# Out projection of a hybrid trunk step: tokens split as 282 and 238 columns, and one product for the high and the low half of the 238

## The chip, the cores and the metric

The kernel runs on one core of a Trainium2 chip. A core has a matrix engine (TensorE, PE in the profile, with PEld for its weight loads), three elementwise engines (VectorE = DVE, ScalarE = ACT, GpSimd = POOL), a sync engine that issues DMAs (SP), an on-chip memory of 128 partitions (SBUF) and an accumulator memory of eight banks of 512 f32 columns (PSUM), into which PE writes. The metric is the device time of one execution in microseconds; the median of three runs is given.

## The reference, cut to what matters

One layer of a hybrid decoder trunk for 512 prompt tokens and 8 sample tokens, all in f32: half-step SwiGLU FFN, a mixer of two head groups, a second half-step FFN, a final norm. The mixer ends with the out projection that the change concerns:

```python
    cat = jnp.concatenate([pool_out, y], axis=-1).astype(h.dtype)
    return cat @ w_out, new_pool, new_conv, h_new.astype(ssm_h0.dtype)
...
        h = h + 0.5 * _swiglu(_rms_norm(h, ffn1_norm[l]), ffn1_w_gate[l], ffn1_w_up[l], ffn1_w_down[l])
        m, p, c, s = _hybrid_mixer(_rms_norm(h, mix_norm[l]), st_pool[l], st_conv[l], st_ssm[l],
...
        h = h + m
        h = h + 0.5 * _swiglu(_rms_norm(h, ffn2_norm[l]), ffn2_w_gate[l], ffn2_w_up[l], ffn2_w_down[l])
```

The model width is 1024 and `w_out` is 1536 x 1024. `pool_out` (512 columns) comes from the pooling heads, `y` (1024) from the SSD heads: two groups of 512 columns, each gated with `silu(z)` and normed by its own RMS before the projection.

## The kernel before, in words

Features lie on the 128 partitions and the NT = 520 tokens on the columns. A product's output tile holds 128 features by up to 512 tokens, so the tokens are taken in two halves of HB = 260 (`HALVES`). To reach f32 accuracy with PE's faster f32r type, weights and inputs are split into a high part (the value rounded to f32r) and a low part (the rest), and each product is three: high weights by high input, high weights by low input, low weights by high input. Input tiles hold both halves, as `cat[:, q, k, tokens]` with q = 0 high, 1 low, and k one of four blocks of 128 features.

The out projection is the function `wout(cat, j, d2, fin)`. j = 0, 1, 2 is the third of the concat: the pooling heads (`catp`), then the two gated SSD groups (`cats[0]`, `cats[1]`; in the trace both are called catg). d2 = 0..3 is a weight unit of 1024 columns, good for two output blocks d of 128 features. For each d and each half b, a bank `wo{j}_{d}{b}` takes twelve products of 260 columns (`mm_low_last`: for four k the two with the high weights, then the four with the low weights), and then VectorE adds the bank to the residual `h[:, d, half]`. These are 3 x 8 x 2 = 48 groups, 576 products and 48 adds. In the last third, `fin` follows the add of the second half: ScalarE squares h for the next norm and scales the input of FFN2 (xg_f), which VectorE and ScalarE then split again into high (xth_f) and low (xtl_f).

Strings set the order in which the code issues the stages. `GATE_PLAN` mixes the thirds "o" (j = 0) and "g" (j = 1) with the rest of the SSD scan and the gates; `LAST_PLAN` is "h0 h2 h1 n0 h3 n1 n2 n3", with the last third (h) and pieces of FFN2's first unit in plain f32 between (n, `fill`; rows P<-xg_f at L311). Within this a scheduler orders each engine's instructions by readiness and priority when the kernel is built; on the chip every engine then runs its own list strictly in that order, and waits there for semaphores of the others. So an add's place in VectorE's list is fixed.

A bank is free for the next group when the adds that read it are done. In the mixer there are eight banks with the tag "ps", which the out projection shares with the scan. Before the last third the pool is released and FFN2's opened, with two banks "ps", two "A" and two pairs "BE"; the groups of the last third use the two "ps" banks in turn (d = 1 uses "A"), and the first of them wait for whatever stood in the same memory before.

What stands on VectorE around the adds: the splits of weights into low parts (rows tlo, wlo_wo, L141: 128x1024), the scan's X and E operations, decays of the sample states (h<-h,cb, L1144), two reciprocals of the gate's RMS (yr, L214) and the low halves of the gated concat (catg, L1339).

Of the kernel before, what the change touches and what calls it, by code (L numbers as in the profile page):

```python
# [13 lines left out]
ALU = mybir.AluOpType  # L14
# [7 lines left out]
NT = SEQ + NS  # L22
HB = NT // 2
HALVES = (slice(0, HB), slice(HB, NT))
KD = D // P
FFN = 2816
KF = FFN // P
# [32 lines left out]
_o = 0  # L60
for _n, _w in (("ffn1_norm", KD), ("mix_norm", KD), ("ffn2_norm", KD), ("final_norm", KD), ("pool_scale", 4),
               ("conv_w", 48), ("conv_b", 12), ("ssd_norm", NX), ("d_skip", NX), ("a_log", NX)):
# [6 lines left out]
def tile_trunk_step(ctx: ExitStack, tc: tile.TileContext, ins: dict, outs: dict):  # L69
    nc = tc.nc  # L70
# [9 lines left out]
    ps = [None]  # L80
# [3 lines left out]

    vx = act.tile([P, NVEC + KD * NT], F32, tag="h", name="h")
    vec = vx[:, :NVEC]
    h = vx[:, NVEC:].rearrange("p (d t) -> p d t", d=KD)

# [61 lines left out]
    def mm3(ps, whi, wlo, xhi, xlo, start, stop, pin=False, **kw):  # L150
# [3 lines left out]
        nc.tensor.matmul(ps, whi, xlo, start=False, stop=False, **kw)  # L154
        nc.tensor.matmul(ps, wlo, xhi, start=False, stop=stop, **kw)  # L155

    def mm_low_last(ps, whi, wlo, xhi, xlo, start, pin=False, **kw):
        for k, w in enumerate(whi):
            for x in (xhi[k], xlo[k]):
                mm = nc.tensor.matmul(ps, w, x, start=start, stop=False, **kw)  # L160
                if pin:
                    tc.keep_in_program_order(mm)
                start = pin = False
        for k, w in enumerate(wlo):
            nc.tensor.matmul(ps, w, xhi[k], start=False, stop=k == len(wlo) - 1, **kw)  # L165

    def ws(w, k, m=P):
        return w[:, k * m : (k + 1) * m]

    def stat(name):  # L170
        return (act.tile([P, NT], F32, tag="acc", name=f"acc_{name}"),
                act.tile([P, NT], F32, tag="r", name=f"r_{name}"))

    def new_x(xp, name):
        xh = xp.tile([P, KD, NT], F32R, tag="xa", bufs=2, name=f"xh_{name}")
        xl = xp.tile([P, KD, NT], F32R, tag="xa", bufs=2, name=f"xl_{name}")
        return xh, xl, *stat(name)
# [29 lines left out]
    def rstd(r, acc, hs, width, name, pin=False):  # L207
        ps = bank(f"psr_{name}")[:, : hs.stop - hs.start]
        for k, sq in enumerate(acc):
            mm = nc.tensor.matmul(ps, ones, sq, start=k == 0, stop=k == len(acc) - 1)  # L210
            if pin:
                tc.keep_in_program_order(mm)
        root = nc.scalar.activation(out=r[:, hs], in_=ps, func=AF.Sqrt, bias=eps, scale=1.0 / width)
        recip = nc.vector.reciprocal(out=r[:, hs], in_=r[:, hs])  # L214
        return root.ins, recip.ins

    def rstds(nx, name, pin=False):
        for b, hs in enumerate(HALVES):
            ends = rstd(nx[3], [nx[2][:, hs]], hs, D, f"{name}{b}", pin)
        return ends  # L220
# [4 lines left out]
    def new_xt(xp, name):  # L225
        return (xp.tile([P, KD // 2, 7, HB], F32R, tag="xth", name=f"xth_{name}"),
                xp.tile([P, KD // 2, 7, HB], F32R, tag="xtl", name=f"xtl_{name}"), *stat(name))
# [43 lines left out]
    class Ffn:  # L271
# [198 lines left out]
        def product(self, f, p):  # L470
# [22 lines left out]
            if self.i == 2:  # L493
                mm_low_last(out[:, :HB], wh, wl, *xs, opens, pin, skip_group_check=True)
            else:
                for j in js:
                    mm3(out[:, :HB], wh[j], wl[j], xs[0][j], xs[1][j], opens and j == 0, j == js[-1],
                        pin=pin and j == 0, skip_group_check=True)
# [93 lines left out]
        def down(self, c, lo, hi, after):  # L592
# [19 lines left out]
            def done(d):  # L612
# [6 lines left out]
                if after is None:  # L619
                    nc.vector.tensor_tensor(out=hd, in0=t, in1=hd, op=ALU.add)  # L620
                    return
                for b, hs in enumerate(HALVES):
                    nc.vector.tensor_tensor(out=h[:, d, hs], in0=t[:, b], in1=h[:, d, hs], op=ALU.add)
# [15 lines left out]
        def down_by_half(self, c, lo, after, wd):  # L639
# [32 lines left out]
            def done(d, b):  # L672
                hs = HALVES[b]
                t = self.wx.tile([P, 2, HB], F32, tag="ac", bufs=3, name=f"th{self.i}_{d}{b}")[:, 0]
                for c in QUARTERS if (d, b) == (KD - 1, 1) else (slice(0, HB),):
                    cs = slice(hs.start + c.start, hs.start + c.stop)
                    nc.vector.scalar_tensor_tensor(out=t[:, c], in0=banks[d, b][:, c], scalar=-0.5, in1=self.nx[3][:, cs],
                                                   op0=ALU.mult, op1=ALU.mult)
                    nc.vector.tensor_tensor(out=h[:, d, cs], in0=t[:, c], in1=h[:, d, cs], op=ALU.add)
                after(d, b, hs)  # L680
# [70 lines left out]
    nx2, xa = [], []  # L751
# [51 lines left out]

    ps[0] = tc.alloc_tile_pool(name="ppm", bufs=8, space=PSUM, reuse_waits="tile")
    mixer(tc, ins, outs, dict(locals()))
    f2["xg"].release()
    xa[0].release()
# [48 lines left out]
    def finish(b):  # L856
        hs, hg, rl, rt, idt = HALVES[b], *res
        acc = last[:, hs]
# [39 lines left out]
def mixer(tc, ins, outs, e):  # L898
    nc = tc.nc
    cst, act, wp, tmp, dr, pool = (e[x] for x in ("cst", "act", "wp", "tmp", "dr", "pool"))  # L900
    ones, queued, squared = e["ones"], e["queued"], tuple(e["added"])
    bank, load_unit, mm3, mm_low_last, ws, v, rstd, rstds, vec, h, nx2, raw_tile, open_f2, fin, fill = (
        e[x] for x in ("bank", "load_unit", "mm3", "mm_low_last", "ws", "v", "rstd", "rstds", "vec", "h", "nx2", "raw_tile",
                       "open_f2", "fin", "fill"))
    xh, xl, _, r = nx2[0]
    xa = e["xa"][0]
# [22 lines left out]
    def inproj(src, name):  # L929
        wh, wl = load_unit(src, D, f"in{name}", squared if name == "bc1" else ())  # L930
        bs = [bank(f"in{name}{b}") for b in range(2)]
        for b, hs in enumerate(HALVES):
            for k in range(KD):
# [18 lines left out]
    dtb = [bank(f"dt{b}") for b in range(2)]  # L952
    for b, hs in enumerate(HALVES):
        for k in range(KD):
# [331 lines left out]
    def wout(cat, j, d2, fin=None):  # L1286
        src, name = ins["w_out"][j, d2], f"wo{j}{d2}"
        if (j, d2) in OUT_LOW_BY_DMA:
            raw = raw_tile(name)
            nc.sync.dma_start(out=raw, in_=src)  # L1290
            wh, wl = e["weight_homes"](1024, name, wp, 3, ("whi", "wlo"))
            e["part_by_dma"](wh, wl, raw, src)
        else:
            wh, wl = load_unit(src, 1024, name, behind.get((j, d2), ()))
        for d in (2 * d2, 2 * d2 + 1):
            for b, hs in enumerate(HALVES):
                if d != 1 or j != 2:
                    ps = bank(f"wo{j}_{d}{b}")
                else:
                    ps = e["ps"][0].tile([P, 512], F32, tag="A", bufs=2, name=f"wo{j}_{d}{b}")  # L1300
                i = range((d % 2) * 4, (d % 2) * 4 + 4)
                mm_low_last(ps[:, :HB], *([ws(w, k) for k in i] for w in (wh, wl)),
                            *([cat[:, q, k, hs] for k in range(4)] for q in range(2)), True)
                nc.vector.tensor_tensor(out=h[:, d, hs], in0=ps[:, :HB], in1=h[:, d, hs], op=ALU.add)  # L1304
                if fin is not None:
                    fin(d, b, hs)

# [48 lines left out]
    def outs_a():  # L1356
# [19 lines left out]
        "B": lambda j: ssd_b(*ssd(j)),  # L1376
        "z": zproj,
        "o": lambda j: wout(catp, 0, j),
        "G": gate,
        "H": gate_out,  # L1380
        "g": lambda j: wout(cats[0], 1, j),
        "h": lambda j: wout(cats[1], 2, j, fin),
        "n": fill,
        "e": lambda j: outs_a(),
# [101 lines left out]
```

## Time and profile before

| what | value |
|---|---|
| runs | 956.82, 953.67, 954.66 us; median 954.66 |
| profiled execution, first to last instruction (its own time as the profile shows it) | 951.9 us, 2.76 below the median |
| granted TensorE clock, mean | 0.997 |
| PE / PEld busy | 942.5 us (99%) / 925.9 us (97%) |
| DVE / ACT / POOL busy | 852.7 (90%) / 635.7 (67%) / 148.3 us (16%) |
| out projection's adds (L1304) | 48, 19.2 us busy, from 532.2 to 609.3 us |
| out projection's products (L160, L165 wo) | from 525.5 to 608.5 us |

A row of a timeline gives the start, the time to the end of the last of the row's instructions, the engine, the line, the operation with output and inputs, the shape, how many (x), and in brackets how long the engine had been idle before and who released it. The duration of a single instruction is longer than the distance to the next one's start, since an engine begins the next before the last is through; the distance ("pitch") is what counts in a full engine. Profile times are those of one execution; the three runs have been timed without it.

### The profile page before, as it was taken

How to read it: one execution, taken by the hardware profiler on the slowest of the kernel's cores; microseconds unless marked ns; L12 is line 12 of the kernel's file. 1: busy time of each engine (PE TensorE's matmuls, PEld its weight loads, DVE VectorE, ACT ScalarE, POOL GpSimd, SP SyncE). 2: the span in 40 equal slices, each digit the busy share in tenths (PEclk: the TensorE clock that was granted, in tenths of full speed). 3: DMA queues.
4: the chain of work that ended last, by engine and by line, in shares of the span. 5: the costliest groups of instructions: out<-in, count | busy, mean ns of one | idle time of the engine just before them, and what ended most of it. 6: DMA issues, size and time to landing. Idle time of an engine off the chain costs nothing.

```text
span 951.9 us, 19681 instructions
## 1 busy us (share of the span) xinstructions
PE 942.5 (99%) x7674; PEld 925.9 (97%) x7674; DVE 852.7 (90%) x1462; ACT 635.7 (67%) x1179; POOL 148.3 (16%) x230
## 2 busy tenths in 40 slices
PE   9999999999999999999999999999999999999996
PEld 8999999999999999999999999999999999999996
DVE  6899899998988688789998998999999999999886
ACT  7777756677566455485668735777776676766774
POOL 0011100100100000046251100111112101122120
PEclk9999999999999999999999999999999999999998
DMA  7666554455553343354264453556666655776552
GB/s 205 187 166 150 143 151 135 115 140 156 134 155 95 86 134 122 92 180 138 91 184 133 141 114 115 138 122 160 163 173 176 163 146 144 171 194 185 145 180 91
DMA packets 53995, 138.35 MB, mean 145 GB/s; under 512 B 7750, under 2 KB 15878, under 8 KB 53902
## 3 DMA queue, kind: packets, MB, share of 16 engines
q1 hardware_dynamic: 39918, 104.19, 34.2%
q0 software_dynamic: 13712, 32.78, 18.7%
q8 instruction: 60, 0.98, 0.4%
q14 instruction: 33, 0.27, 0.1%
q10 hardware_dynamic: 272, 0.13, 0.0%
HBM read 129.74 MB, written 7.34 MB: 144 GB/s over the span
## 4 chain that ended last, share of the span: by engine, by line
PE 44%; DVE 2%; issue 1%; POOL 1%; DMA 1%; ACT 1%; DVEq 0%; ACTq 0%; POOLq 0%
PE A L160 8%; PE BE L160 6%; PE wo L160 5%; PE A L165 4%; PE BE L165 3%; PE wo L165 2%; PE P L311 1%; PE dh L155 1%; PE dh L151 1%; PE dh L154 1%; POOL zs L1068 1%; PE inz L151 1%; PE inz L154 1%; PE inz L155 1%; DMA room<-in_state_ssm 1%
## 5 line engine op out<-in xcount | busy, mean ns | idle before, releaser
L504 ACT COPY ac<-A 128x260 f32<-128x260 f32 x85 | 31.6, 372 | 35.4 <-PE A L155 17.3
L433 DVE TENSOR_TENSOR s<-raw 128x1024 f32<-128x1024 f32 x39 | 47.6, 1222 | 4.4 <-DMA raw<-in_w2gu 2.8
L504 ACT COPY ac<-BE 128x260 f32<-128x260 f32 x41 | 15.4, 376 | 33.6 <-PE BE L165 17.7
L151 PE MATMUL inx<-xh_mx,whi_inx 128*128 128x260 f32 x112 | 31.8, 284 | 0.0
L154 PE MATMUL inx<-xl_mx,whi_inx 128*128 128x260 f32 x112 | 31.6, 282 | 0.0
L155 PE MATMUL inx<-xh_mx,wlo_inx 128*128 128x260 f32 x112 | 31.6, 282 | 0.0
L1027 DVE SCALAR_TENSOR_TENSOR A<-U,h,A 128x544 f32<-128x544 f32 x36 | 29.0, 807 | 1.6 <-ACT A L1025 1.2
L311 PE MATMUL P<-x,raw 128*128 128x260 f32 x128 | 28.9, 385 | 0.2 <-DMA raw<-in_w1gu 0.2
L311 PEld LDWEIGHTS P<-x,raw 128*128 128x128 f32 x128 | 24.4, 192 | 4.2 <-DMA raw<-in_w1gu 0.6
L160 PE MATMUL wo<-catg,whi_wo 128*128 128x260 f32 x192 | 27.4, 285 | 0.0
L1193 ACT ACTIVATE so<-br,sxdt 128x128 f32<-128x128 f32 x64 | 22.8, 376 | 5.8 <-DVE room L1195 5.2
L160 PEld LDWEIGHTS wo<-catg,whi_wo 128*128 128x128 f32 x192 | 24.8, 188 | 0.2
L139 ACT CAST thi<-raw 128x1024 fp32r<-128x1024 f32 (+1 forms) x14 | 14.2, 1012 | 15.7 <-PE wo L160 4.8
L1304 DVE TENSOR_TENSOR h<-wo,h 128x260 f32<-128x260 f32 x48 | 19.2, 422 | 5.0 <-PE wo L165 4.7
L252 DVE TENSOR_TENSOR gs<-gq,gs 128x780 fp32r<-128x780 f32 (+1 forms) x28 | 23.3, 831 | 0.0
L151 PE MATMUL inz<-xh_mx,whi_inz 128*128 128x260 f32 x80 | 23.0, 287 | 0.0
L154 PE MATMUL inz<-xl_mx,whi_inz 128*128 128x260 f32 x80 | 22.7, 284 | 0.0
L155 PE MATMUL inz<-xh_mx,wlo_inz 128*128 128x260 f32 x80 | 22.6, 283 | 0.0
L251 ACT CAST gs<-gq 128x780 fp32r<-128x780 f32 (+1 forms) x28 | 20.6, 735 | 1.2 <-DVE gq L555 0.8
L151 PEld LDWEIGHTS inx<-xh_mx,whi_inx 128*128 128x128 f32 x112 | 21.1, 188 | 0.2 <-issue 0.2
L160 PE MATMUL A<-xth_f,qs 128*128 128x260 f32 x84 | 21.2, 283 | 0.0
L160 PE MATMUL A<-xtl_f,qs 128*128 128x260 f32 x84 | 21.2, 284 | 0.0
(3140 smaller groups left out, 4382.9 us busy)
## 6 DMA issues: line engine op xcount, KB each, us to landing
raw<-in_w2gu SPq DMA_DIRECT2D x44, 512.0 KB, 4.4
raw<-in_w1gu SPq DMA_DIRECT2D x41, 512.0 KB, 4.3
raw<-in_w_in SPq DMA_DIRECT2D x24, 512.0 KB, 3.7
raw<-in_w1d SPq DMA_DIRECT2D x16, 512.0 KB, 4.6
raw<-in_w2d SPq DMA_DIRECT2D x16, 512.0 KB, 4.6
raw<-in_w_out SPq DMA_DIRECT2D x12, 512.0 KB, 3.5
ab<-scr_acs SPq DMA_DIRECT2D x8, 512.0 KB, 5.5
h<-in_state_ssm SPq DMA_DIRECT2D x16, 256.0 KB, 3.7
```

What stands on the lines that cost most here:

```text
L151: first = nc.tensor.matmul(ps, whi, xhi, start=start, stop=False, **kw)
L154: nc.tensor.matmul(ps, whi, xlo, start=False, stop=False, **kw)
L155: nc.tensor.matmul(ps, wlo, xhi, start=False, stop=stop, **kw)
L160: mm = nc.tensor.matmul(ps, w, x, start=start, stop=False, **kw)
L165: nc.tensor.matmul(ps, w, xhi[k], start=False, stop=k == len(wlo) - 1, **kw)
L251: cast = nc.scalar.copy(hi, s)
L252: low = nc.vector.tensor_tensor(out=lo, in0=s, in1=hi.bitcast(F32), op=ALU.subtract)
L311: mm = nc.tensor.matmul(self.banks[f, u][b][:, :HB], ws(self.raw[f][:, u], j + 4 * q), xg[:, slot[q]], start=j == q == 0, stop=j == 3 and ...
L433: nc.vector.tensor_tensor(out=s1, in0=diag, in1=up0, op=ALU.add)
L504: self.copied = nc.scalar.copy(keep, out[:, :HB]).ins
L1027: nc.vector.scalar_tensor_tensor(out=A[:, :n], in0=U[:, j : j + n], scalar=w(j), in1=A[:, :n], op0=ALU.mult, op1=ALU.add)
L1193: nc.scalar.activation(out=o[:, q], in_=br, func=AF.Copy, scale=sxdt[:, j, b : b + 1]))
```

## The change

The tokens of the out projection are no longer cut at 260 but at 282 (`SPANS`, `WIDE`, `NARROW` = 238). The first part is computed as before with 282 columns. For the second part one product takes the high weights with the high and the low half of the rows side by side, 2 x 238 = 476 columns into one bank (`mm_both_low_last`), and the four low weights' products of 238 columns are added onto the first 238 of these. The bank then holds two partial sums, and VectorE adds the one and then the other to `h`. So a pair of halves has 20 products and not 24, with the same 6,240 columns, and three adds and not two. Of the rest of the kernel only line numbers change: `mm_low_last` is L176 and L181 now, `mm_both_low_last` L186 and L188, the adds L1332; `mm_both` and `join` are defined and not called.

```diff
--- before.py
+++ after.py
@@ -22,6 +22,9 @@
 NT = SEQ + NS
 HB = NT // 2
 HALVES = (slice(0, HB), slice(HB, NT))
+WIDE = 282
+NARROW = NT - WIDE
+SPANS = (slice(0, WIDE), slice(WIDE, NT))
 KD = D // P
 FFN = 2816
 KF = FFN // P
@@ -154,6 +157,19 @@
         nc.tensor.matmul(ps, whi, xlo, start=False, stop=False, **kw)
         nc.tensor.matmul(ps, wlo, xhi, start=False, stop=stop, **kw)

+    def mm_both(ps, whi, wlo, x, start, stop, pin=False):
+
+        n = x.shape[-1]
+        first = nc.tensor.matmul(ps[:, : 2 * n].rearrange("p (q t) -> p q t", q=2), whi, x, start=start, stop=False)
+        if pin:
+            tc.keep_in_program_order(first)
+        nc.tensor.matmul(ps[:, :n], wlo, x[:, 0], start=False, stop=stop)
+
+    def join(ps, home):
+        n = home.shape[-1]
+        nc.scalar.copy(home, ps[:, n : 2 * n])
+        return nc.vector.tensor_tensor(out=ps[:, :n], in0=ps[:, :n], in1=home, op=ALU.add)
+
     def mm_low_last(ps, whi, wlo, xhi, xlo, start, pin=False, **kw):
         for k, w in enumerate(whi):
             for x in (xhi[k], xlo[k]):
@@ -163,6 +179,13 @@
                 start = pin = False
         for k, w in enumerate(wlo):
             nc.tensor.matmul(ps, w, xhi[k], start=False, stop=k == len(wlo) - 1, **kw)
+
+    def mm_both_low_last(ps, whi, wlo, x):
+        n = x[0].shape[-1]
+        for k, w in enumerate(whi):
+            nc.tensor.matmul(ps[:, : 2 * n].rearrange("p (q t) -> p q t", q=2), w, x[k], start=k == 0, stop=False)
+        for k, w in enumerate(wlo):
+            nc.tensor.matmul(ps[:, :n], w, x[k][:, 0], start=False, stop=k == len(wlo) - 1)

     def ws(w, k, m=P):
         return w[:, k * m : (k + 1) * m]
@@ -899,8 +922,8 @@
     nc = tc.nc
     cst, act, wp, tmp, dr, pool = (e[x] for x in ("cst", "act", "wp", "tmp", "dr", "pool"))
     ones, queued, squared = e["ones"], e["queued"], tuple(e["added"])
-    bank, load_unit, mm3, mm_low_last, ws, v, rstd, rstds, vec, h, nx2, raw_tile, open_f2, fin, fill = (
-        e[x] for x in ("bank", "load_unit", "mm3", "mm_low_last", "ws", "v", "rstd", "rstds", "vec", "h", "nx2", "raw_tile",
+    bank, load_unit, mm3, mm_both, join, mm_low_last, mm_both_low_last, ws, v, rstd, rstds, vec, h, nx2, raw_tile, open_f2, fin, fill = (
+        e[x] for x in ("bank", "load_unit", "mm3", "mm_both", "join", "mm_low_last", "mm_both_low_last", "ws", "v", "rstd", "rstds", "vec", "h", "nx2", "raw_tile",
                        "open_f2", "fin", "fill"))
     xh, xl, _, r = nx2[0]
     xa = e["xa"][0]
@@ -1293,15 +1316,20 @@
         else:
             wh, wl = load_unit(src, 1024, name, behind.get((j, d2), ()))
         for d in (2 * d2, 2 * d2 + 1):
-            for b, hs in enumerate(HALVES):
+            for b, hs in enumerate(SPANS):
                 if d != 1 or j != 2:
                     ps = bank(f"wo{j}_{d}{b}")
                 else:
                     ps = e["ps"][0].tile([P, 512], F32, tag="A", bufs=2, name=f"wo{j}_{d}{b}")
                 i = range((d % 2) * 4, (d % 2) * 4 + 4)
-                mm_low_last(ps[:, :HB], *([ws(w, k) for k in i] for w in (wh, wl)),
-                            *([cat[:, q, k, hs] for k in range(4)] for q in range(2)), True)
-                nc.vector.tensor_tensor(out=h[:, d, hs], in0=ps[:, :HB], in1=h[:, d, hs], op=ALU.add)
+                if b:
+                    mm_both_low_last(ps, *([ws(w, k) for k in i] for w in (wh, wl)), [cat[:, :, k, hs] for k in range(4)])
+                else:
+                    mm_low_last(ps[:, :WIDE], *([ws(w, k) for k in i] for w in (wh, wl)),
+                                *([cat[:, q, k, hs] for k in range(4)] for q in range(2)), True)
+                n = hs.stop - hs.start
+                for q in range(1 + b):
+                    nc.vector.tensor_tensor(out=h[:, d, hs], in0=ps[:, q * n : q * n + n], in1=h[:, d, hs], op=ALU.add)
                 if fin is not None:
                     fin(d, b, hs)
```

How it stands on VectorE in the first third (o0), where the first adds meet the scan's X operations; wo0_01 is the bank of third 0, block d = 0, second half. Before:

```order
L1304 TENSOR_TENSOR h_69<-wo0_00_6668,h_69 128x260
L1304 TENSOR_TENSOR h_69<-wo0_01_6682,h_69 128x260
L1276 SCALAR_TENSOR_TENSOR X_4306<-X_4306,h_69,E21_6344 128x128 x4
L1144 TENSOR_TENSOR h0_61_6649<-h0_61_6649,cb61_6647 128x512
L1144 TENSOR_TENSOR h0_71_6658<-h0_71_6658,cb71_6656 128x512
L1304 TENSOR_TENSOR h_69<-wo0_10_6696,h_69 128x260
L1304 TENSOR_TENSOR h_69<-wo0_11_6710,h_69 128x260
L141 TENSOR_TENSOR tlo_3833<-raw_74,thi_3832 128x1024
```

Now:

```order
L1332 TENSOR_TENSOR h_69<-wo0_00_6668,h_69 128x282
L1332 TENSOR_TENSOR h_69<-wo0_01_6682,h_69 128x238
L1299 SCALAR_TENSOR_TENSOR X_4306<-X_4306,h_69,E21_6344 128x128 x4
L1167 TENSOR_TENSOR h0_61_6649<-h0_61_6649,cb61_6647 128x512
L1167 TENSOR_TENSOR h0_71_6658<-h0_71_6658,cb71_6656 128x512
L1332 TENSOR_TENSOR h_69<-wo0_01_6682,h_69 128x238
L1332 TENSOR_TENSOR h_69<-wo0_10_6693,h_69 128x282
L1332 TENSOR_TENSOR h_69<-wo0_11_6707,h_69 128x238
L144 TENSOR_TENSOR tlo_3833<-raw_74,thi_3832 128x1024
```

The second part of wo0_01 does not follow the first but stands behind the X operations and the two decays.

VectorE around the last low halves of the second gated concat (catg1, L1339 and now L1367), which the last third multiplies. Before:

```order
L1304 TENSOR_TENSOR h_69<-wo1_50_7153,h_69 128x260
L1304 TENSOR_TENSOR h_69<-wo1_51_7167,h_69 128x260
L1304 TENSOR_TENSOR h_69<-wo1_60_7186,h_69 128x260
L1339 SCALAR_TENSOR_TENSOR catg1_7109<-zs_5724,h_69,catg1_7109 128x520 x2
L1304 TENSOR_TENSOR h_69<-wo1_61_7200,h_69 128x260
L1339 SCALAR_TENSOR_TENSOR catg1_7109<-zs_5724,h_69,catg1_7109 128x520 x2
L141 TENSOR_TENSOR tlo_3833<-raw_74,thi_3832 128x1024
L1304 TENSOR_TENSOR h_69<-wo1_70_7214,h_69 128x260
L1304 TENSOR_TENSOR h_69<-wo1_71_7228,h_69 128x260
L141 TENSOR_TENSOR wlo_wo21_7400<-raw_74,whi_wo21_7399 128x1024
L1304 TENSOR_TENSOR h_69<-wo2_00_7267,h_69 128x260
```

Now:

```order
L1332 TENSOR_TENSOR h_69<-wo1_60_7144,h_69 128x282
L1367 SCALAR_TENSOR_TENSOR catg1_7073<-zs_5724,h_69,catg1_7073 128x520 x2
L1332 TENSOR_TENSOR h_69<-wo1_61_7158,h_69 128x238
L1367 SCALAR_TENSOR_TENSOR catg1_7073<-zs_5724,h_69,catg1_7073 128x520
L1332 TENSOR_TENSOR h_69<-wo1_51_7128,h_69 128x238
L1367 SCALAR_TENSOR_TENSOR catg1_7073<-zs_5724,h_69,catg1_7073 128x520
L144 TENSOR_TENSOR tlo_3833<-raw_74,thi_3832 128x1024
L1332 TENSOR_TENSOR h_69<-wo1_70_7169,h_69 128x282
L1332 TENSOR_TENSOR h_69<-wo1_71_7183,h_69 128x238
L1332 TENSOR_TENSOR h_69<-wo1_61_7158,h_69 128x238
L144 TENSOR_TENSOR wlo_wo21_7340<-raw_74,whi_wo21_7339 128x1024
L1332 TENSOR_TENSOR h_69<-wo1_71_7183,h_69 128x238
```

The second part of wo1_51 has come between the last two low halves, and the second part of wo1_61 stands behind the low part of a weight (tlo) and two more adds.

PE at the second group of the last third, wo2_01. Before:

```order
L160 MATMUL wo2_00_7267<-catg1_7109,whi_wo20_7263 128x260 [waits DVE_49]
L165 MATMUL wo2_00_7267<-catg1_7109,wlo_wo20_7264 128x260 x4
L160 MATMUL wo2_01_7281<-catg1_7109,whi_wo20_7263 128x260 x8
L165 MATMUL wo2_01_7281<-catg1_7109,wlo_wo20_7264 128x260 x4
L160 MATMUL wo2_10_7296<-catg1_7109,whi_wo20_7263 128x260 [waits DVE_49]
```

Now:

```order
L176 MATMUL wo2_00_7219<-catg1_7073,whi_wo20_7215 128x282 [waits DVE_49]
L181 MATMUL wo2_00_7219<-catg1_7073,wlo_wo20_7216 128x282 x4
L186 MATMUL wo2_01_7233<-catg1_7073,whi_wo20_7215 128x476 [waits DVE_49,PE_49]
L186 MATMUL wo2_01_7233<-catg1_7073,whi_wo20_7215 128x476 x3
L188 MATMUL wo2_01_7233<-catg1_7073,wlo_wo20_7216 128x238 x4
```

The group had no wait of its own; now its first product waits for VectorE, and by the value of the semaphore for the second part of wo1_61. In the first third, the first product of wo0_20 waits in the same way for the second part of wo0_01 (before, for its only add), and in the last third a narrow block waits for both parts of the block two before in its bank. On PE outside the out projection only a few pieces of the fills (P<-xg_f) move behind the next product's group; POOL's and SP's lists are the same, and on ACT a few neighbours change places.

## The prediction

> **What bounds the kernel now.** I read the page first, then the busy time by stretches of 10 us around the out projection (525 to 610 us), then PE and VectorE there in order of time. The page gives the span and the engines' shares:
>
> ```profile
> span 951.9 us, 19681 instructions
> PE 942.5 (99%) x7674; PEld 925.9 (97%) x7674; DVE 852.7 (90%) x1462; ACT 635.7 (67%) x1179; POOL 148.3 (16%) x230
> ```
>
> PE is busy 942.5 of 951.9 us, so over the whole program the time is the sum of PE's work: whatever makes PE stop is added, and shorter PE work is gained. The same by stretches (columns: stretch, length, busy time and number of instructions of PE, PEld, DVE, ACT, POOL, then the granted clock, the DMA share and GB/s):
>
> ```profile
> 530.00:540.00 10.00, 10.00 (x83) 8.95 (x82) 10.00 (x17) 9.66 (x26) 1.19 (x1) 1.00 0.30 90
> 540.00:550.00 10.00, 10.00 (x86) 10.00 (x85) 10.00 (x26) 7.25 (x12) 0.90 (x1) 1.00 0.57 157
> 550.00:560.00 10.00, 10.00 (x86) 10.00 (x85) 10.00 (x19) 4.39 (x6) 0.85 (x1) 1.00 0.74 175
> 560.00:570.00 10.00, 10.00 (x83) 9.88 (x82) 7.94 (x12) 1.79 (x3) 0.00 (x0) 1.00 0.19 61
> 570.00:580.00 10.00, 10.00 (x86) 10.00 (x85) 10.00 (x19) 4.60 (x6) 0.00 (x0) 1.00 0.26 77
> 580.00:590.00 10.00, 10.00 (x78) 9.71 (x77) 6.81 (x12) 6.55 (x9) 0.00 (x0) 1.00 0.44 135
> ```
>
> The stage that is changed has two full engines: PE 10.00 in every row, and VectorE (DVE) 10.00 in four of six. Its only air is 10 − 7.94 = 2.06 us and 10 − 6.81 = 3.19 us. The change makes PE's instructions fewer and DVE's more, so it must be costed on both.
>
> **PE's side.** For each pair of halves (24 of them) 24 products of 260 columns become 12 of 282, 4 of 476 and 4 of 238. Columns: 24 × 260 = 6,240, and 12 × 282 + 4 × 476 + 4 × 238 = 6,240. Only a price per product, not per column, can be saved. PE in order of time, and the dt projection with its narrow weights:
>
> ```profile
> 553.94 1.12 PE L160 MATMUL wo<-catg,whi_wo 128*128 128x260 f32 x8
> 554.90 0.64 PE L165 MATMUL wo<-catg,wlo_wo 128*128 128x260 f32 x4
> 555.37 1.12 PE L160 MATMUL wo<-catg,whi_wo 128*128 128x260 f32 x8
> ...
> L957 PEld LDWEIGHTS dt<-xh_mx,whi_w x16: 120/121/123, 351.8 to 355.9; 128*48 128x48 f32 x16
> L956 PEld LDWEIGHTS dt<-xl_mx,whi_w x14: 94/94/98, 352.1 to 355.7; 128*16 128x16 f32 x14
> ...
> 352.31 0.28 PE L957 MATMUL dt<-xh_mx,whi_w 128*48 128x260 f32 x1
> 352.43 0.28 PE L956 MATMUL dt<-xl_mx,whi_w 128*16 128x260 f32 x1
> 352.55 0.28 PE L957 MATMUL dt<-xh_mx,whi_w 128*48 128x260 f32 x1
> ...
> 584.91 1.91 PE L311 MATMUL P<-xg_f,raw 128*128 128x260 f32 x8
> ...
> 608.51 3.67 PE L311 MATMUL P<-xg_f,raw 128*128 128x260 f32 x16
> ```
>
> A group of twelve takes 555.37 − 553.94 = 1.43 us, 119 ns for one 260-column product, or 0.46 ns a column. The plain f32 products of the fills (L311, each recorded as two) take (3.67 − 1.91) / 8 = 220 ns a record of 260 columns. If such a record is two passes of the columns, one pass is 110 ns, and the other 9 to 10 ns of the 119 are a price per product. With 48- and 16-column weights (loads of 121 and 94 ns) the pitch is still 120 ns, so the weight load does not set it. Saved are 96 products × 0 to 10 ns = 0 to 1 us. I take the upper end, 40 ns a pair, since the two kinds of product differ by just that; it counts only where PE isn't made to wait afterwards. The Trainium skill ("TensorE: Matmul & The Clock Gate", Back-to-back issue gap) gives an isolated product N / 2.4 + 2.5 ns, by which 96 fewer would save 0.24 us and a 260-column product would take 110.8 ns; the trace's 119 speaks against those figures here.
>
> **DVE's side.** 48 adds of 260 columns become 24 of 282 and 48 of 238. The two parts of a narrow block are added in turn, the second reads the h that the first wrote. DVE at the first groups, and two dependent operations later:
>
> ```profile
> 530.99 0.68 DVE L1269 TENSOR_TENSOR hst<-pst,hst 128x512 f32<-128x512 f32 x1
> 531.59 0.68 DVE L1273 TENSOR_TENSOR E<-yd,E 128x512 f32<-128x512 f32 x1
> 532.19 0.75 DVE L1304 TENSOR_TENSOR h<-wo,h 128x260 f32<-128x260 f32 x2
> 532.86 1.91 DVE L1276 SCALAR_TENSOR_TENSOR X<-X,h,E 128x128 f32<-128x128 f32 x4
> 534.70 1.28 DVE L1144 TENSOR_TENSOR h<-h,cb 128x512 f32<-128x512 f32 x2
> 535.90 0.75 DVE L1304 TENSOR_TENSOR h<-wo,h 128x260 f32<-128x260 f32 x2
> 536.57 1.21 DVE L141 TENSOR_TENSOR tlo<-raw,thi 128x1024 fp32r<-128x1024 f32 x1
> ...
> 602.91 0.42 DVE L240 SCALAR_TENSOR_TENSOR xd_f<-xd_f,xg_f 128x260 f32<-128x260 f32 x1
> 603.37 0.43 DVE L242 SCALAR_TENSOR_TENSOR xd_f<-xd_f,xg_f 128x260 f32<-128x260 f32 x1
> ```
>
> Two adds take 536.57 − 535.90 = 0.67, one 0.335 to 0.338; 512 columns from a bank take 531.59 − 530.99 = 0.60. The slope is 0.265 / 252 = 1.05 ns a column, so an add of 282 costs 0.361 and one of 238 0.315. New DVE work: 24 × 0.361 + 48 × 0.315 − 48 × 0.338 = +7.6 us, against 5.25 us of air. Where the parts are neighbours, the second costs up to 603.37 − 602.91 − 0.338 = 0.12 more. Until its second part is added, the narrow block's bank isn't free.
>
> *First stop, o0.* In the order, the second part of block 1 of d=0 stands behind four X operations and two decays of h, and the third pair's first product now waits for it. Those end at 535.90, the widths shift that by (0.361 + 0.315 − 0.67) = 0, and the second part ends a duration of 0.40 later (a 260 shows 0.75 − 0.335 = 0.42): 536.30. PE began that group here:
>
> ```profile
> 535.11 1.23 PE L160 MATMUL wo<-catp,whi_wo 128*128 128x260 f32 x8
> ```
>
> So PE stops for 536.30 − 535.11 = 1.2 us. Nothing hides it; PE's order is fixed there. Bounds: 0, if a bank were free after all, and 1.3 with two savings of 40 ns ahead of it.
>
> *Second stop, the start of the last third.* Here DVE's three pauses, the end of the second gated concat, and the two products that need it:
>
> ```profile
> 562.75 0.43 DVE L1304 TENSOR_TENSOR h<-wo,h 128x260 f32<-128x260 f32 x1 [0.46 <-PE wo L165]
> 564.17 0.43 DVE L1304 TENSOR_TENSOR h<-wo,h 128x260 f32<-128x260 f32 x1 [1.00 <-PE wo L165]
> 565.20 3.42 DVE L214 RECIPROCAL yr<-yr 128x260 f32<-128x260 f32 x2 [0.60 <-ACT yr L213]
> ...
> 575.40 1.42 DVE L1339 SCALAR_TENSOR_TENSOR catg<-zs,h,catg 128x520 fp32r<-128x520 f32 x2
> 576.74 1.22 DVE L141 TENSOR_TENSOR tlo<-raw,thi 128x1024 fp32r<-128x1024 f32 x1
> 577.88 0.76 DVE L1304 TENSOR_TENSOR h<-wo,h 128x260 f32<-128x260 f32 x2
> ...
> 576.31 1.12 PE L160 MATMUL wo<-catg,whi_wo 128*128 128x260 f32 x8
> 577.75 1.11 PE L160 MATMUL wo<-catg,whi_wo 128*128 128x260 f32 x8
> ```
>
> Ahead of the third reciprocal stand 24 adds before, 12 of 282 and 24 of 238 now: 12 × 0.361 + 24 × 0.315 − 24 × 0.338 = 3.78 us later, of which the pauses 0.46 + 1.00 + 0.60 = 2.06 take up: 1.72. From there to the last low half of the concat 6 adds become 3 wide and 5 narrow ones: 3 × 0.361 + 5 × 0.315 − 6 × 0.338 = 0.63. DVE reaches the low of the next weight 2.35 late, at 579.09. The first group (576.31) waits for the last low half and is about 2.4 late. The second (577.75) now waits for a bank that falls free only with the second part of the sixth block, behind that weight low (577.88 − 576.74 = 1.14), a wide and a narrow add and its own 0.40: 579.09 + 1.14 + 0.36 + 0.31 + 0.40 = 581.30, 3.55 us after 577.75. This lateness is absolute: the first stop and PE's savings up to here lie in it.
>
> *Behind it.* Eight more pairs, less the first group, save about 7 × 0.040 = 0.3 us. Near the end, with two banks in turn, the last block waits for both parts of the block two before: its two adds and the split of 128x1024 between them (1.15) take 0.17 + 0.315 + 1.13 + 0.40 = 2.0 us, while the product between gives 1.44: +0.56. The last block's h, from which FFN2's first input is scaled and split, is complete one narrow add (0.315) and one operation put between (0.46, the pitch at 602.91) later: +0.8. FFN2 follows at a full PE, and nothing is made up there. Instructions of POOL and SP keep their order, and ACT's move by a place; their cost is 0, with their waits for DVE counted above.
>
> Sum: 3.55 − 0.3 + 0.56 + 0.8 = **+4.6 us**. The profiled execution is 951.9 long and goes to 956.5; the median of the runs, 954.66, lies 2.76 above that span, so the time is 959.3. Ends: lower +2.9 (the second stop only the first group's 2.4, half the tail), upper +9 (all 24 second parts 0.12 dearer, 2.9 us, and 1.5 of the 2.06 us of pauses not usable, since PE, for which DVE waits there, is late itself).
>
> **The rivals.**
> *A, the adds are mostly hidden.* For it: DVE's 3.19 us between 580 and 590, and the wait at 577.75 that only pays if no bank is free. Then the tail and a piece of the second stop remain, 0 to +2.8: 955 to 957.4. Against it: DVE's 10.00 in the three rows from 530 to 560.
> *B, faster: PE's pitch is set per product, by the weight load, not by columns.* PEld is at 97%. Then 282 and 238 cost 119 as 260 does, a 476 what its columns take, 476 × 110 / 260 = 201: a pair costs 16 × 119 + 4 × 201 = 2,708 ns and not 24 × 119 = 2,856, with 24 × 148 = 3.6 us saved: 951.1. It decides only if DVE stops PE for less than about 0.7 us. Against it: the dt rows, whose light loads gain nothing. The Trainium skill says in the same section that in a stream of loads and products both set the spacing, with about 81 ns at 128 columns and 131 at 512; an estimate by a straight line between these gives 6.2 us saved, but also 98 ns at 260, where the trace has 119.
> *C, a 238-column product runs at a lower rate.* No f32r product here is narrower than 260 columns, so the price is bounded by the plain f32 product, 2 × 220 ns for 260: at that rate a 238 costs 2 × 220 × 238 / 260 = 403 and not 109, 96 × 0.294 = +28 us, and DVE, with more time, stops PE no more: 982. At half the rate, 96 × 0.10 = +10: 965. Nothing in the profile speaks for it, and nothing excludes it.
>
> **How the numbers follow.** The measurement can tell about 0.3%, 2.9 us: below 951.8 is faster, above 957.5 slower. My case (957.5 to 963.7) gets 0.72, A 0.09, B 0.05, C 0.14 (most of it at the full f32 price). Slower is my case and C, 0.86; same is A, 0.09; faster is B, 0.05. The range 955.5 to 966 holds my case, most of A and the half rate of C, 0.8 together.
>
> **What would show it.** PE: a first gap ahead of the third pair of o0 of about 1.2 us released by an add of 238; gaps of 2 to 4 us in all at the first two groups of the last third; DVE at 10.00 from 530 to 580; pitches near 129, 212 and 107 ns for 282, 476 and 238. Adds near 0.44 and 0.40 long. I am wrong if PE runs through these places, if the 238 products stand 200 ns or more apart, or if PE's time for a pair falls by more than 0.1 us.

## The result and the profile after

The changed kernel takes 959.58 us (median of 4 runs, 958.80 to 963.15) and the kernel before 954.16 us beside it (4 runs). The ratio is 1.0058 with a 95% interval from 1.0035 to 1.008: 5.4 us slower, between 3.3 and 7.6. Taken again in the first group of experiments, the ratio was 1.0046 (1.0033 to 1.0059), 4.4 us. The forecast was 959.3, +4.6 us. One execution of e6 below took 1544.76 us at a granted clock of 0.556, where all others had 0.993 or more; the ratios leave it out, and without it e6's median is 956.58 and not 956.96.

The execution that was profiled first is not a typical one: its span is 961.3 us, the spans of the other three runs are 956.9 to 958.4. Part of that lies outside the change. It had lost 1.5 us before the out projection began, and 1.2 us behind it, at 675 us in FFN2, to a weight transfer that took 8.7 us where 4.2 is usual. So I read the terms from a second profile of the same kernel (e1 below), whose span is 956.1. Its page, first lines:

```profile
span 956.1 us, 19529 instructions
PE 943.8 (99%) x7578; PEld 923.9 (97%) x7578; DVE 859.5 (90%) x1486; ACT 635.4 (66%) x1179; POOL 148.4 (16%) x230
```

PE has 96 instructions fewer and is not less busy (943.8 against 942.5); VectorE (DVE) has 24 more and is 6.8 us busier. The busy time by stretches, of the profile taken first, shows PE below 10.00 where it was full in every row before:

```profile
530.00:540.00 10.00, 7.79 (x58) 6.24 (x58) 10.00 (x20) 9.10 (x23) 1.08 (x1) 1.00 0.23 67
...
560.00:570.00 10.00, 10.00 (x69) 9.51 (x68) 10.00 (x22) 3.00 (x5) 0.00 (x0) 1.00 0.33 105
570.00:580.00 10.00, 10.00 (x70) 9.54 (x69) 10.00 (x17) 3.54 (x5) 0.00 (x0) 1.00 0.18 55
580.00:590.00 10.00, 8.73 (x59) 8.07 (x58) 8.32 (x16) 4.04 (x6) 0.00 (x0) 1.00 0.31 105
```

VectorE's air between 560 and 570 (7.94 before) is gone. PE in order of time, from e1: the rows with an idle time in brackets are all its stops between 500 and 620 us.

```profile
536.17 1.27 PE L176 MATMUL wo<-catp,whi_wo 128*128 128x282 f32 x8 [1.37 <-DVE h L1332]
...
578.09 1.27 PE L176 MATMUL wo<-catg,whi_wo 128*128 128x282 f32 x8 [0.29 <-DVE h L1332]
...
580.88 1.11 PE L186 MATMUL wo<-catg,whi_wo 128*128 128x476 f32 x4 [0.98 <-DVE h L1332]
...
611.12 1.11 PE L186 MATMUL wo<-catg,whi_wo 128*128 128x476 f32 x4 [0.48 <-DVE h L1332]
```

All four are released by an add (L1332), at the third pair of o0, the first two groups of the last third and the last block (block here means one half of the tokens for one d). A bracket holds only what remains of a wait after PE's modelled end, so the sum of the brackets, 3.1, is less than what was lost; the starts tell the loss. VectorE beside them, from e1, with the adds that release the first three stops:

```profile
535.64 1.06 DVE L1332 TENSOR_TENSOR h<-wo,h 128x238 f32<-128x238 f32 x3
...
577.55 0.40 DVE L1332 TENSOR_TENSOR h<-wo,h 128x238 f32<-128x238 f32 x1
577.87 0.75 DVE L1367 SCALAR_TENSOR_TENSOR catg<-zs,h,catg 128x520 fp32r<-128x520 f32 x1
578.54 1.22 DVE L144 TENSOR_TENSOR tlo<-raw,thi 128x1024 fp32r<-128x1024 f32 x1
579.67 1.07 DVE L1332 TENSOR_TENSOR h<-wo,h 128x282 f32<-128x282 f32 x3
```

The first add of the group at 535.64 is the second part of o0's first narrow block; PE starts at 536.17, when it is through. The add at 577.55 is the second part of wo1_51; it ends at 577.95 and PE starts at 578.09. The third of the group at 579.67 is the second part of wo1_61; it ends at 580.74 and PE starts at 580.88.

### The profile page after: what moved, and what is told of

Read it like the earlier page. It is cut to its first block, busy times and chain, and to the rows that moved or that the text cites. A ratio compares the mean times of both kernels' runs of the same rounds, so it can differ in the third digit from the quotient of the medians.

```text
span 961.3 us, 19529 instructions
## 1 busy us (share of the span) xinstructions
PE 945.5 (98%) x7578; PEld 924.2 (96%) x7578; DVE 859.2 (89%) x1486; ACT 635.1 (66%) x1179; POOL 149.1 (16%) x230
## 4 chain that ended last, share of the span: by engine, by line
PE 33%; DVE 11%; DMA 3%; issue 2%; POOL 1%; ACT 1%; DVEq 0%; ACTq 0%
PE A L176 7%; PE BE L176 5%; PE A L181 3%; PE BE L181 3%; DMA raw<-in_w2gu 2%; DVE h L1332 2%; PE dh L158 1%; PE dh L154 1%; PE dh L157 1%; PE P L334 1%; DMA cb<-scr_bc 1%; POOL zs L1091 1%; PE wo L186 1%; PE wo L176 1%; DVE h L1167 1%
## 5 line engine op out<-in xcount | busy, mean ns | idle before, releaser
L1332 DVE TENSOR_TENSOR h<-wo,h 128x238 f32<-128x238 f32 (+1 forms) x72 | 27.0, 408 | 3.6 <-PE wo L188 2.2
L176 PE MATMUL A<-xth_f,qs 128*128 128x260 f32 x84 | 21.2, 283 | 0.0
L176 PE MATMUL A<-xtl_f,qs 128*128 128x260 f32 x84 | 21.2, 284 | 0.0
L158 PEld LDWEIGHTS inx<-xh_mx,wlo_inx 128*128 128x128 f32 x112 | 21.1, 188 | 0.0
L157 PEld LDWEIGHTS inx<-xl_mx,whi_inx 128*128 128x128 f32 x112 | 21.1, 188 | 0.0
```

The lines of the kernel that those rows point to most:

```text
L1332: nc.vector.tensor_tensor(out=h[:, d, hs], in0=ps[:, q * n : q * n + n], in1=h[:, d, hs], op=ALU.add)
```

## The experiments

For each run the table gives the ratio to the kernel before, in runs on the same chip, and how long the stage lasts in its profile: from the start of the out projection's first product to that of the last one of FFN2's column sums (psr_f). The stage is read from rows like these (the latter's first start belongs to FFN1), here of before and of e1: it is 614.7 − 525.5 = 89.2 us before and 618.7 − 525.1 = 93.6 in e1:

```profile
L160 PE MATMUL wo<-catp,thi x64: 277/282/389, 525.5 to 551.9; 128*128 128x260 f32 x64
L210 PE MATMUL psr_f<-acc_f,ones x8: 382/382/383, 22.8 to 614.7; 128*128 128x260 f32 x8
```

```profile
L176 PE MATMUL wo<-catp,thi x32: 290/293/400, 525.1 to 551.5; 128*128 128x282 f32 x32
L233 PE MATMUL psr_f<-acc_f,ones x8: 382/382/383, 23.1 to 618.7; 128*128 128x260 f32 x8
```

| kernel | ratio (95%) | stage, against 89.2 us |
|---|---|---|
| the change, first profile | 1.0058 (1.0035 to 1.0080) | 94.7, +5.5 |
| e1 the change again | 1.0046 (1.0033 to 1.0059) | 93.6, +4.4 |
| e2 one add | 1.0005 (0.9995 to 1.0016) | 89.7, +0.5 |
| e3 before, with 24 adds | 1.0053 (1.0041 to 1.0066) | 93.5, +4.3 |
| e4 second add from on-chip memory | 1.0049 (1.0031 to 1.0066) | 91.4, +2.2 |
| e7 the same again | 1.0045 (1.0033 to 1.0057) | 91.5, +2.3 |
| e5 second add in thirds 0 and 1 | 1.0050 (1.0038 to 1.0063) | 92.9, +3.7 |
| e6 second add in the last third | 1.0033 (1.0021 to 1.0046) | 90.5, +1.3 |
| e8 second add on GpSimd | 1.0123 (1.0109 to 1.0137) | 99.9, +10.7 |
| e9 cut at 392 and 128 | 1.0075 (1.0060 to 1.0090) | 93.7, +4.5 |
| e10 the same, one add | 1.0060 (1.0044 to 1.0075) | 94.3, +5.1 |

My theory was that VectorE's extra adds, late in a full list, stop PE. The first rival was that PE's new products cost the time; the second, that a price per product is saved and VectorE hides its part; and within my own theory it was open what is due to the load and what to the banks that the second parts hold.

**e1, the changed kernel again.**

> The changed kernel once more, for a second profile: the first profiled execution (span 961.3) was longer than the timed ones (956.9 to 958.4). All theories: median 958.8 to 960.3, and the same stops of PE: ahead of the third pair of o0 about 1.2 us, at the first two groups of the last third together 2 to 4 us, at the last block about 0.5 us.

Measured 958.79 us (957.96 to 960.24), with the four stops shown above. It agrees, if the stops are counted by PE's starts (3.5 us at the first two groups, see the next section) and not by the brackets.

**e2, one add.** VectorE's part of the change is taken away, PE's is kept; the sum lacks the low half of the narrow blocks' rows.

```diff
-                for q in range(1 + b):
-                    nc.vector.tensor_tensor(out=h[:, d, hs], in0=ps[:, q * n : q * n + n], in1=h[:, d, hs], op=ALU.add)
+                nc.vector.tensor_tensor(out=h[:, d, hs], in0=ps[:, :n], in1=h[:, d, hs], op=ALU.add)
```

> The changed products, but only the first 238 columns of a narrow bank are added (the low half of the rows is left out of the narrow blocks' sum), so VectorE has 48 adds again with as many columns as before. Theory 1 (VectorE's 24 extra adds and the banks they hold cost the time): 953.5 to 955.5, no stop of PE. Theory 2 (PE itself, the 476-column product with two runs of columns or the 238-column one, costs the time): 957 or more. Rival of the prediction that products have a fixed price that is saved: 951 to 953.

Measured 955.32 us, ratio 1.0005; no row of PE between 500 and 640 us has an idle time before it. So the products of 282, 476 and 238 columns cost no more than 1.5 us, and save at most 0.5: the rival of a saved price falls with its 3.6 us, and so does that of a slow 238-column product.

**e3, the adds alone.** PE's part is undone and VectorE's kept, in the kernel before:

```diff
                 nc.vector.tensor_tensor(out=h[:, d, hs], in0=ps[:, :HB], in1=h[:, d, hs], op=ALU.add)
+                if b:
+                    nc.vector.tensor_tensor(out=h[:, d, HB + 22 :], in0=ps[:, 22:HB], in1=h[:, d, HB + 22 :], op=ALU.add)
```

> The kernel before with its products of 260 columns and one add of 238 more after the add of each second half, read from the same bank (the sum gets a part twice). VectorE's list is that of the changed kernel nearly row by row. Theory 1: 958 to 960.5, with the stops of PE at the same three places. Theory 2: 954 to 955.5.

Measured 959.29 us, ratio 1.0053, and PE stops at the same first three places with the old products:

```profile
536.00 1.23 PE L160 MATMUL wo<-catp,whi_wo 128*128 128x260 f32 x8 [1.28 <-DVE h L1306]
...
577.99 1.20 PE L160 MATMUL wo<-catg,whi_wo 128*128 128x260 f32 x8 [0.62 <-DVE h L1306]
...
580.68 1.22 PE L160 MATMUL wo<-catg,whi_wo 128*128 128x260 f32 x8 [1.02 <-DVE h L1306]
```

At the last block it does not stop; it loses the time behind it instead, with brackets of 0.28 us at 615.95 and of 0.55 and 0.89 at 620.83 and 622.10, where PE waits for FFN2's scaled and split input. e2 and e3 together decide the main question: the 24 adds alone cost as much as the whole change, the products nothing that the times show.

**e4 and e7, load without held banks.** The second add keeps its place in VectorE's list and its length (0.39 to 0.41 us in e7, where the adds of e1 have a median of 0.40), but reads elsewhere; the low half's product is left out of the sum:

```diff
+                nc.vector.tensor_tensor(out=h[:, d, hs], in0=ps[:, :n], in1=h[:, d, hs], op=ALU.add)
+                if b:
+                    nc.vector.tensor_tensor(out=h[:, d, hs], in0=cat[:, 1, 0, hs].bitcast(F32), in1=h[:, d, hs], op=ALU.add)
```

> The changed kernel, but the second add of a narrow block reads 238 columns of the rows' low half in on-chip memory and not the bank (the low half's product is left out of the sum), so that VectorE's list keeps its length and order and the bank is free after the first add. Load alone: the stop ahead of the third pair of o0 goes, and of that at the last third the 2.3 us for the last low half of the concat stays: 956.5 to 958.5. If held banks are all that costs: 953.5 to 955.5. If load is all and banks nothing: 958.8 to 960.3.

> The kernel with the second add from on-chip memory once more: its times scattered from 956.3 to 961.3, and its profile shows the stage 3.2 us longer than before, against 4.9 in the changed kernel. If held banks cost 1 to 1.5 us: 956.8 to 958.2. If load alone costs all: 958.8 to 960.3. Profile: no stop ahead of the third pair of o0, but one of about 0.8 at its narrow block, on the bank of the norm's column sums.

Measured 958.97 and 957.97 us, ratios 1.0049 and 1.0045: the first lies in the band for "load is all", the second in that for held banks of 1 to 1.5 us. PE in e7, with its only two stops in the stage:

```profile
537.82 1.13 PE L186 MATMUL wo<-catp,whi_wo 128*128 128x476 f32 x4 [0.87 <-ACT yr L236]
...
577.80 1.08 PE L176 MATMUL wo<-catg,whi_wo 128*128 128x282 f32 x7
579.08 0.40 PE L176 MATMUL wo<-catg,whi_wo 128*128 128x282 f32 x1 [0.21 <-DVE catg L1368]
579.32 0.69 PE L181 MATMUL wo<-catg,wlo_wo 128*128 128x282 f32 x4
579.84 1.03 PE L186 MATMUL wo<-catg,whi_wo 128*128 128x476 f32 x4
```

The stop ahead of the third pair is gone, but one block later PE runs into another wait, for the bank of the gate's column sums, which ScalarE's square root (yr) frees: the stop has moved and shrunk a little. At the last third PE waits for the last low half of the concat, as the sum said for the load alone, and no longer for a bank. In the profiles the stage is 2.1 to 2.2 us shorter than in e1: without PE's 0.5 us (e2) that leaves 1.7 to 1.8 to the load and gives 2.1 to 2.2 to the held banks. The times don't show it: the ratios of e1 and e7 differ by 0.0001 (1.0033 to 1.0059 against 1.0033 to 1.0057), which leaves room for 1 us and hardly for 2. In its profile e7 also takes longer from the stage's end to its own, 339.1 us against 337.4 in e1; it was 337.2 before and 339.6 in the change's first profile, so this part differs between executions of one kernel too. So the load alone costs something between 1.7 us and nearly all of it; how much of the whole the held banks cost stays open.

**e5 and e6, the second add in some thirds only.**

```diff
-                for q in range(1 + b):
+                for q in range(1 + (b and j < 2)):     # e5;  e6: j == 2
```

> The changed kernel with the second add only in the first two thirds (in the last third the low half of the rows is left out of the narrow blocks' sum). By my sum the lateness of the second stop stays, 3.55 us, and of the tail's 1.4 us nothing is left: +3.3, 957 to 958.5. If the last third's own adds cost most: 954 to 956.

> The changed kernel with the second add only in the last third (in the first two thirds the low half of the rows is left out of the narrow blocks' sum). By my sum no stop at o0 or at the start of the last third, the tail's 0.56 and 0.8 stay: +1.0 to +1.4, 955.3 to 956.5. If the last third's own adds cost most: 957 or more.

Measured 958.53 us, ratio 1.0050, and 956.96, ratio 1.0033. In the profiles, e5 has the three earlier stops and not the one at the last block, and its stage is 3.7 us longer; e6 has only that last one, and its stage is 1.3 longer. 3.7 + 1.3 − 0.5 (PE's part, in both) = 4.5 is e1's 4.4: the two terms of my sum stand apart and add up. The times are higher than these by about 1 us for e5 and 1.8 for e6, with intervals of 1.2 us to each side, and e6's lies above the 956.5 that was expected. Of e6's 1.8 us 0.6 is lost right behind the stage, in the tail that the next section describes. In e5's profile 1.1 us of it is this wait in FFN2, the last step of a chain that goes back to a weight transfer of 8.43 us (raw<-in_w2gu in the chain of waits):

```profile
671.41 0.39 PE L176 MATMUL BE<-xth_f,shi_6c 128*128 128x260 f32 x1 [1.10 <-ACT BE L527]
```

In e1 that transfer takes 7.5 us, and PE waits 0.17 us at the same product. Such a delay is not a property of the change that I could show; for e6 the remaining 1.2 us aren't explained.

**e8, the second add on other engines.** Complete, but ScalarE copies the second part out of the bank and GpSimd (POOL) adds it:

```diff
+                nc.vector.tensor_tensor(out=h[:, d, hs], in0=ps[:, :n], in1=h[:, d, hs], op=ALU.add)
+                if b:
+                    part = tmp.tile([P, HB], F32, tag="ta", name=f"part{j}_{d}")[:, :n]
+                    nc.scalar.copy(part, ps[:, n : 2 * n])
+                    nc.gpsimd.tensor_tensor(out=h[:, d, hs], in0=part, in1=h[:, d, hs], op=ALU.add)
```

> The changed kernel, complete; ScalarE copies the second part of a narrow block from the bank to on-chip memory and GpSimd adds it to h, so VectorE has 48 adds again with the columns of before. Theory 1: the stops on VectorE at o0 and at the last third's start go, the tail keeps about 1 us, since the last block's h now passes through ScalarE and GpSimd: 954.5 to 957. Theory 2 (PE's own products cost it): 958 or more. Also 958 or more, if GpSimd's adds or ScalarE's copies are themselves late.

Measured 965.38 us, ratio 1.0123: the remedy is worse than the change. GpSimd's add takes 0.6 to 1.6 us, and PE waits 3.22 us for a copy of ScalarE that itself waited for VectorE's add:

```profile
L1335 POOL TENSOR_TENSOR h<-part,h x24: 604/982/1607, 535.4 to 619.8; 128x238 f32<-128x238 f32 x24
```

```profile
576.68 0.61 PE L188 MATMUL wo<-catg,wlo_wo 128*128 128x238 f32 x4
580.51 2.25 PE L176 MATMUL wo<-catg,whi_wo 128*128 128x282 f32 x8 [3.22 <-ACT part L1334]
582.56 1.14 PE L181 MATMUL wo<-catg,wlo_wo 128*128 128x282 f32 x4
```

```profile
580.10 0.36 ACT L1334 COPY part<-wo 128x238 f32<-128x238 f32 x1 [1.92 <-DVE h L1331]
```

What such a stop does to the clock stands in the last section.

**e9 and e10, other widths.** The second add of a narrower block is cheaper for VectorE; for PE it asks whether a price by the column holds further down.

```diff
-WIDE = 282
+WIDE = 392
```

> The changed kernel with the tokens cut at 392 and 128 in place of 282 and 238: four products of 256 and four of 128 columns in a narrow block, 6,240 columns a pair as before. VectorE's extra work falls from 7.6 to 24 x 0.477 + 48 x 0.200 - 48 x 0.338 = 4.8 us. If PE's price is by the column only (0.46 ns in all widths so far): 955.5 to 957.5, between before and the change. If a narrow product has a floor (the weight load's), so that 128 columns take some 100 ns and not 59: 4 us more, 959 to 962.

> The same widths of 392 and 128 with one add for each block (the low half of the rows is left out of the narrow blocks' sum), so that VectorE has no extra work and PE's price stands alone. By the column only: 953.5 to 955.5, as before. With a floor of some 100 ns for 128 columns: 957 to 960, PE busy throughout and the rows of the 128-column products 100 ns apart.

Measured 960.95 and 959.59 us, ratios 1.0075 and 1.0060. PE in e10:

```profile
539.54 1.65 PE L176 MATMUL wo<-catp,whi_wo 128*128 128x392 f32 x8
541.03 0.88 PE L181 MATMUL wo<-catp,wlo_wo 128*128 128x392 f32 x4
541.75 0.63 PE L186 MATMUL wo<-catp,whi_wo 128*128 128x256 f32 x4
542.22 0.56 PE L188 MATMUL wo<-catp,wlo_wo 128*128 128x128 f32 x4
542.61 1.65 PE L176 MATMUL wo<-catp,whi_wo 128*128 128x392 f32 x8
```

392 columns take (541.03 − 539.54) / 8 = 186 and (541.75 − 541.03) / 4 = 180 ns and 256 take 118, 0.46 to 0.47 ns a column; 128 take (542.61 − 542.22) / 4 = 98 and not 59. So a product of 128 columns has a price beyond its columns, a floor: 96 products × 39 ns = 3.7 us, most of e10's 5.7. And e9, with VectorE's extra adds on top, is only 1.4 us slower than e10, without a stop of PE in its stage, which isn't longer than e10's (93.7 against 94.3, with one wait of 0.25 us for a weight transfer): with fewer added columns and a slower PE VectorE's adds are hidden there, as the sum for a slow narrow product had assumed.

No kernel here beats the one before, and the runs give no reason to look for it in this change: PE's part saves nothing.

## Why the prediction was right, point by point

**The time.** 959.58 against 959.3, inside the range, and the case that was given 0.72. The difference to before, 5.4 or 4.4 us, stands against 4.6. That the time is met to 0.3 us is partly luck: the four runs of the changed kernel spread from 958.80 to 963.15, and the kernel before measured 954.16 beside them and not the 954.66 from which the forecast went.

**PE's side: this term was wrong.** I took 9 to 10 ns of every product as a fixed price and saved 40 ns a pair. PE in e1:

```profile
556.38 1.21 PE L176 MATMUL wo<-catg,whi_wo 128*128 128x282 f32 x8
557.43 0.70 PE L181 MATMUL wo<-catg,wlo_wo 128*128 128x282 f32 x4
557.96 1.04 PE L186 MATMUL wo<-catg,whi_wo 128*128 128x476 f32 x4
558.85 0.61 PE L188 MATMUL wo<-catg,wlo_wo 128*128 128x238 f32 x4
559.29 0.94 PE L176 MATMUL wo<-catg,whi_wo 128*128 128x282 f32 x6
```

A pair takes 559.29 − 556.38 = 2.91 us, and 24 × 0.119 = 2.86 before (2.87 between the starts of most pairs there). The widths give 131 to 133, 222 and 110 ns, where 129, 212 and 107 were forecast; that is 0.46 to 0.47 ns a column in each. So the price is by the column, nothing is saved, and in the gated thirds 0.04 us a pair is even lost, 0.6 us in sixteen pairs, which fits e2's +0.5 us in the stage; in the first third a pair takes 2.87 us as before. The step that failed is the reading of plain f32 (220 ns as two passes of 110) as a price by column for f32r: the 9 to 10 ns above it are no fixed part of an f32r product, since the widths from 238 to 476 share one price by the column. The error was small because in my sum the saving counted for only 0.3 us.

**First stop.** Forecast 1.2 us: PE at 536.30 and not 535.11. In e1 it starts at 536.17 with a stage that began 0.37 us earlier (525.13 against 525.50): 1.06 + 0.37 = 1.4 us. VectorE's row at 535.64 shows the order's place of the second part as forecast.

**Second stop.** Forecast 2.4 us at the first group, 3.55 at the second. In e1 578.09 − 576.31 = 1.78 and 580.88 − 577.75 = 3.13, with the same 0.37 on top 2.2 and 3.5. VectorE reaches the next weight's low part at 578.54, 2.2 late in the same way, where the sum had 2.35. For the first group the sum named the last low half of the concat. In e1 the trace names an add, the second part of wo1_51, which ends 0.67 us before that low half does (577.95 against 578.62). Without it, in e7, the group starts at once and its eighth product waits for the low half, so the low half keeps the group nearly as late: the low weights' products start 579.32 − 525.50 = 53.82 us after the stage's start there and 579.21 − 525.13 = 54.08 in e1. At the second group the held bank makes the larger difference: this group starts at 579.84 − 525.50 = 54.34 in e7, 2.1 us later than before, and at 580.88 − 525.13 = 55.75 in e1, 3.5 later. The sum had 2.4 for the load and 3.55 with the bank. e5 gives its three stops and PE's part together 3.7.

**The tail.** Forecast −0.3 + 0.56 + 0.8. The stop at the last block has a bracket of 0.48 in e1 and in e6; by PE's starts it is 0.64 (in e1 611.12 against 609.95 + 0.53 for the four products before). The sum had set the old group's 1.44 us as the product between; twelve of 282 columns at its own 129 ns are 1.55, which makes 0.45 of the 0.56. e6's stage is 1.3 longer, 0.8 without PE's part. The forecast 0.8 for the late input of FFN2 does not lie in the stage, but right behind it. Here first of before, then of e1:

```profile
617.17 0.29 PE L160 MATMUL A<-xth_f,shi_1d 128*128 128x260 f32 x1
```

```profile
621.11 0.39 PE L176 MATMUL BE<-xtl_f,shi_1c 128*128 128x260 f32 x1 [0.28 <-DVE xtl_f L275]
...
621.81 0.29 PE L176 MATMUL A<-xth_f,shi_1d 128*128 128x260 f32 x1
```

From the stage's end to the product A<-xth_f,shi_1d it is 617.17 − 614.7 = 2.5 us before and 621.81 − 618.7 = 3.1 in e1, 0.6 more (e6 3.1 too, e2 and e5 2.7). So in e1's profile the change costs 4.4 in the stage and 0.6 behind it, 5.0, against 4.6: the stops were forecast to 0.2 us, PE's products lose 0.5 us and save nothing, and the late input costs 0.4 to 0.6 and not 0.8.

**What the sum did not tell.** It took the held bank at o0 as the cause of the first stop, with a lower bound of 0 if a bank were free; e4 and e7 show that another bank's wait stands right behind it (0.77 and 0.87 us). And the rows of DVE do not say what the weights' transfers in FFN2 make of a shift; that moves single executions by a microsecond, as much as a term of the sum.

**The rivals.** A, hidden adds: excluded by e3. B, a price per product: excluded by e2 in its size of 3.6 us. A price per product does exist, but below the widths of this change: e10 shows it at 128 columns. That the weight load sets it is not shown. C, a slow 238-column product: excluded by the 110 ns above.

## What to carry to other kernels

Count the work that a change gives to the second-busiest engine before counting what it saves on the first: here 7.6 us of VectorE's time by the sum (6.8 by the page) in a stage with 5 us of air became 4.4 to 5.4 us, and PE's 96 fewer instructions nothing, since the columns stayed the same. A partial sum left in a bank for a second pass is held for as long as the second pass stands in its engine's list, and that place is to be looked up in the built order, not in the code. A term that is read from two kinds of instruction needs a row of the same kind at another width, and where the trace has none, the range should carry it.

## What the runs showed of the hardware

In e8 PE's pause of 3.22 us cost more than itself. The clock granted to PE fell to half before it was over (columns: stretch, length, busy times, then the clock):

```profile
577.00:580.00 3.00, 0.29 (x3) 0.10 (x1) 3.00 (x6) 1.19 (x2) 1.54 (x1) 0.93 0.00 0
580.00:582.00 2.00, 1.49 (x6) 1.49 (x7) 1.14 (x2) 0.36 (x1) 1.07 (x1) 0.50 0.65 244
582.00:584.00 2.00, 2.00 (x10) 1.94 (x9) 0.26 (x1) 0.00 (x0) 0.00 (x0) 0.50 0.80 219
584.00:586.00 2.00, 2.00 (x9) 1.80 (x8) 0.19 (x1) 0.00 (x0) 0.00 (x0) 0.50 0.15 61
586.00:588.00 2.00, 2.00 (x15) 1.97 (x15) 0.47 (x2) 0.56 (x2) 0.61 (x1) 0.89 0.00 0
```

A mean of 0.93 over the first row puts the fall from 1.00 to 0.50 at about 579.6, one of 0.89 over the last the rise at about 586.4. So PE worked 5.9 us, from 580.51 on, at half the clock, where eight products of 282 took 2.05 us and not 1.05; that is some 3 us on top of the pause. The pauses of 1.67 us and less in the changed kernel left the clock at 1.00. The Trainium skill ("TensorE: Matmul & The Clock Gate", What's actually happening) says that the clock halves after an idle window of about 3.4 us and doubles again after as long a busy one. The trace agrees in the two levels and not in the times: the clock fell about 2.5 us after the end of the last columns, 576.68 + 4 × 0.110 = 577.12, with 0.9 us of the pause still to come, and it rose only 5.9 us after PE had started again. It is one pause; what the limit is, no run here shows.

An f32r product of 128 columns with 128-column weights took 98 ns, and one of 238 to 476 columns 0.46 to 0.47 ns a column: somewhere between 128 and 238 columns the price by the column ends. The same page of the Trainium skill (Back-to-back issue gap) gives about 81 ns for a stream of loads and products at 128 columns; in f32r here it is 98.
